# Two paces instead of one for the side work of a hybrid layer: 0.15 beside the recurrence, 0.55 from the last query projection on, where it was 0.43 throughout

## The chip, the cores and the metric

The kernel runs on one core of a Trainium2 chip. The metric is the device time of one execution in microseconds; lower is better. Engines are named as the profile names them: PE is TensorE (matmuls; PEld its weight loads), DVE is VectorE, ACT is ScalarE, POOL is GpSimd, SP is SyncE, which issues nearly all DMA.

## The reference

One inference step of a two-layer encoder over 592 tokens (16 meta tokens, 512 of a prompt, 64 of a second request that has a cache of 256 keys). Each layer computes `x + W_out(sum_b sigmoid(G_b(n)) * P_b(branch_b(n) * silu(gate_b(n))))` with `n = RMSNorm(x)`, over three branches:

```python
# A: an indexer scores all keys, each query keeps the best k, softmax over those
s_idx = relu(einsum('bthd,bsd->bths', qi, ki))
score = einsum('bth,bths->bts', wi, s_idx)       # 4 indexer heads, then top_k(score, k)
attn  = softmax over the kept keys of q.k / 8    # 8 heads of 64; k = 128, second request 80
# B: causal convolution of width 4, then a gated linear recurrence
h_t = a_t * h_(t-1) + sqrt(1 - a_t**2) * (i_t * x_t)
# C: trailing means over 2, 4, 8 and 16 frames less the token, a linear map per group
```

Queries and keys get a rotary embedding on the first quarter of each head. Keys, values, indexer keys and the states of B and C are outputs too.

## The kernel before, in words

**Projections.** The main work is a sequence of projections, emitted in a fixed order. A weight chunk of 128 x 1024 is loaded by SP (six chunks ahead at most), split by ACT and DVE into a high and a low part (`prefetch`, L190 and L191), and multiplied in three products per block of 128 (L267, `mm3`). `c_project` takes one chunk in two pieces of 296 tokens (288 in layer 1 where the meta tokens are not needed any more), 24 matmuls a piece; `psa` gives three PSUM accumulators, so a piece's result must be taken out before the third piece after it starts. After each piece it calls `spend(3 * nk * n / 2.4)`, the piece's nominal nanoseconds at the full clock: 2960 for eight blocks of 296.

**The main order in a layer**: values and indexer keys (`t_project`), two indexer queries (QI), four recurrence inputs (XB), four keys (K), four queries (Q), four gates of the recurrence (GB), the first mix (`mix(1, 0, y)`: eight sigmoid gates and the branch's output projection), four pairs of pooling input and pooling gate (XC, GC, with `pool_group`), the second mix, `side.drain()`, four gates of the attention (GA), the third mix, and the output projection. Keys and queries pass through `rope`: a shuffle on DVE (L364), two multiplications on POOL (L365, L366), an addition on DVE (L367).

**Side work** is written as generators, each of which emits some instructions and yields their cost in nanoseconds. Two queues hold them. `side_lru` (rate 0.4) has the recurrence of the four channel groups, `lru(g)`, added after each XB. `side` has the attention's work. At each `spend(ns)` a queue's credit grows by `ns * rate`, and steps are emitted as long as the credit is positive. A queue works strictly in order; `drain()` emits all that is left. This sets the order in which the program is written. A scheduler then places the instructions on each engine by this order and its own estimate of when they are ready, and an engine executes its list in order.

**`index(j)`** is the indexer for queries of block j (0 to 3: 128 prompt queries against `w = 16 + 128 * (j + 1)` keys; 4: the second request against 320). Four steps of cost `1.1 * w` compute one head's scores on PE (L445, in two PSUM tiles `pq`), which DVE (L448 for the first head, L452 after a rectifier on ACT) adds up in `sc`, of which there is one buffer. Then 16 rounds (10 for j = 4) of cost `2.1 * w + 140` each take the eight largest with `max` (L461) and strike them out with `match_replace` (L462), and a last step of cost `w` turns what was struck out into an additive `bias` (L465, two buffers).

**`attend(j)`** uses that bias: per pair of heads logits on PE (L514; L510 for j = 4), bias and maximum on DVE (L518), exponential on ACT (L524), division on POOL (L527), transposes on PE (L542), their copies on DVE and ACT, the product with the values (L557), and at the end an addition on DVE (L576). Its cost is `2.5 * w` a step, eight steps and 300 (four and 300 for j = 4). `attend_meta` (layer 0 only, cost 4700) does the meta tokens (L606 and on); it reads the rotated queries and keys.

The queue `side` gets `index(4)`, `index(0)` and `index(1)` after QI, and after Q: `attend_meta`, `attend(4)`, `attend(0)`, `index(2)`, `attend(1)`, `index(3)`, `attend(2)`, `attend(3)`. Their costs are 9,848, 7,856 and 12,848 ns, and then 4,700, 3,500, 3,180, 17,840, 5,740, 22,832, 8,300 and 10,860 ns, 76,952 in all. Before, the queue's rate is 0.43 all the time.

Of the kernel before, what the change touches and what calls it, by code (L numbers as in the profile page):

```python
# [34 lines left out]
NRAW = 3  # L35
NSPL = 3
RATE_LRU = 0.4
RATE_ATT = 0.43


class Side:
# [26 lines left out]
def build(ctx, tc, ap):  # L68
# [56 lines left out]

    side = Side(RATE_ATT)
    side_lru = Side(RATE_LRU)
# [159 lines left out]
    def c_project(ch, nk, src, pieces, evac, w=None, off=0, stride=128):  # L287

        if w is None:
            w = take(ch)  # L290
        hi, lo, _ = w[0]
        sh, sl = src
        for i, (c0, n) in enumerate(pieces):
            p = psa.tile([128, 512], F32, name="acc", tag="acc")
            pairs = []
            for k in range(nk):
                wh = hi[:, k * stride + off:k * stride + off + 128]
                wl = lo[:, k * stride + off:k * stride + off + 128]
                a, b = sh[:, k, c0:c0 + n], sl[:, k, c0:c0 + n]
                pairs += [(wh, a), (wh, b), (wl, a)]  # L300
            mm3(p[:, :n], pairs)
            evac(i, c0, n, p[:, :n])
            spend(3 * nk * n / 2.4)
# [4 lines left out]
    def layer(l, xn, x_src, last):  # L308
# [51 lines left out]
        def rope(x, c0):  # L360

            r = x.shape[0]
            t = ep.tile([128, NT], F32, name="rt", tag="e")
            nc.vector.stream_shuffle(t[:r, c0:], x[:, c0:], SWAP)  # L364
            nc.gpsimd.tensor_tensor(t[:r, c0:], t[:r, c0:], rope_s[:r, c0:], op=ALU.mult)  # L365
            nc.gpsimd.tensor_tensor(x[:, c0:], x[:, c0:], rope_c[:r, c0:], op=ALU.mult)  # L366
            nc.vector.tensor_tensor(x[:, c0:], x[:, c0:], t[:r, c0:], op=ALU.add)  # L367

        def rotated(ch, dst, pieces):
            def ev(i, c0, n, p):  # L370
                nc.scalar.activation(dst[:, c0:c0 + n], p, AF.Copy)
            c_project(ch, 8, xn, pieces, ev)
            rope(dst, pieces[0][0])
# [44 lines left out]
        def kspan(j):  # L418

            w = NM + 128 * (j + 1)  # L420
            if w <= 512:
                return [(0, w)]
            return [(0, w // 2), (w // 2, w // 2)]

        def index(j):
            sample = j == 4
            rows = 128
            q0 = NP if sample else NM + 128 * j
            w = 320 if sample else NM + 128 * (j + 1)
            sc = tmp.tile([128, 528], F32, name="sc", tag="sc")  # L430
            spans = [(0, 320)] if sample else kspan(j)
            nq = 64 if sample else 128
            for par in range(2):
                o = 64 * par
                for z in range(0, 128, nq):
                    nc.gpsimd.tensor_copy(qiz[o:o + 64, par::2, z:z + nq], QI[o:o + 64, 0:2, q0:q0 + nq])
            for h in range(4):
                q = qiz[:, h]
                for a, n in spans:
                    p = psq.tile([128, 512], F32, name="pq", tag="qk")  # L440
                    if sample:
                        nc.tensor.matmul(p[:, 0:256], lhsT=q, rhs=kx, start=True, stop=True)
                        nc.tensor.matmul(p[:, 256:320], lhsT=q, rhs=QI[:, 2, NP:NT], start=True, stop=True)
                    else:
                        nc.tensor.matmul(p[:, :n], lhsT=q, rhs=QI[:, 2, a:a + n], start=True, stop=True)  # L445
                    wh = wq[:rows, j, h:h + 1]
                    if h == 0:
                        nc.vector.tensor_scalar(sc[:rows, a:a + n], p[:rows, :n], 0.0, wh, op0=ALU.max, op1=ALU.mult)  # L448
                    else:
                        r = tmp.tile([128, 400], F32, name="rel", tag="rel")  # L450
                        nc.scalar.activation(r[:rows, :n], p[:rows, :n], AF.Relu)
                        nc.vector.scalar_tensor_tensor(sc[:rows, a:a + n], r[:rows, :n], wh, sc[:rows, a:a + n],  # L452
                                                       op0=ALU.mult, op1=ALU.add)
                yield w * 1.1
            if not sample:
                nc.gpsimd.memset(sc[0:64, w - 64:w], MASKED)  # L456
            r0 = 64 if j == 0 else 0
            rr = slice(r0, rows)
            m8 = sm.tile([128, 8], F32, name="m8", bufs=2)
            for _ in range(10 if sample else 16):  # L460
                nc.vector.max(m8[rr], sc[rr, :w])  # L461
                nc.vector.match_replace(sc[rr, :w], m8[rr], sc[rr, :w], TAKEN)  # L462
                yield w * 2.1 + 140
            b = lp.tile([128, 528], BF16, name="bias", tag="bias")
            nc.vector.tensor_scalar(b[rr, :w], sc[rr, :w], TAKEN, -1.0e30, op0=ALU.not_equal, op1=ALU.mult)  # L465
            if j == 0:
                nc.vector.memset(b[0:64, 0:w - 64], 0.0)
                nc.vector.memset(b[0:64, w - 64:w], -1.0e30)
            bias[j] = b
            yield w  # L470
# [311 lines left out]
        last_values()  # L782
        for i in range(2):
            rotated(s["c"][C_QI + i], QI[:, i], FULL)
        side.add(index(4))
        side.add(index(0))
        side.add(index(1))
# [6 lines left out]
        for i in range(4):  # L794
            rotated(s["c"][C_Q + i], QK[:, i], PIECES)
        side_lru.drain()
        if not last:
            side.add(attend_meta())
        side.add(attend(4))
# [88 lines left out]
    for t, (c0, rows) in enumerate(TILES):  # L888
        ss = sm.tile([128, 3], F32, name=f"ss{t}", bufs=1)
        for h in range(2):  # L890
            sumsq(x[t], rows, ss, h, 512 * h, 512 * h + 512)
        norm_T(x[t], rows, c0, rstd_of(ss, 2, rows), gb_t[0], *xn, xg=scale_g(x[t], rows, gb_t[0]) if t else None)
    xn = layer(0, xn, ap["xin"], False)
    layer(1, xn, x1, True)


# [73 lines left out]
```

## Time and profile before

| | us |
|---|---|
| median of three runs | 1247.98 |
| lowest and highest run | 1245.59 and 1248.61 |
| the profiled execution | 1246.41 |
| its span, first to last instruction | 1244.6 |

The profiled execution is 1.57 us below the median, and its span 1.8 us shorter than its own time. Layer 0 takes about the first half of the span, layer 1 the second. In the rows below, busy time is that of the profile: matmuls are pipelined, and a busy PE can hold more or fewer of them in the same time, so their count stands beside it. The clock column is the granted share of TensorE's clock: 1.00 is 2.4 GHz, 0.50 is 1.2 GHz.

### The profile page before, as it was taken

What the parts mean: (1) busy time and instruction counts of PE and PEld (TensorE: products, weight loads), DVE (VectorE), ACT (ScalarE), POOL (GpSimd) and SP (SyncE); (2) the same over time, 40 slices, a digit from 0 to 9 for tenths busy, and PEclk for the clock granted to TensorE, in tenths of its full rate; (3) what the DMA queues carried; (4) which work ended last, traced back from release to release, by engine and by line L of the source; (5) the groups of instructions that cost most, each with busy time, mean ns of one, the idle gap of its engine ahead of it and who ended that gap; (6) DMA issues with size and microseconds to landing.
All of it is one profiled execution on the core that took longest, in us unless ns stands there. A gap on an engine that the chain in (4) does not pass through costs nothing.

```text
span 1244.6 us, 21856 instructions
## 1 busy us (share of the span) xinstructions
PE 1214.7 (98%) x8780; PEld 1185.9 (95%) x8780; DVE 740.2 (59%) x1532; ACT 470.5 (38%) x931; POOL 333.6 (27%) x435
## 2 busy tenths in 40 slices
PE   5999899999999999999999998999999999999997
PEld 5999899999999999999999998899999999999997
DVE  6368996756964335343363789959497543344333
ACT  5336454333333322332343444543423432233223
POOL 7042453131134410011012334441221442101120
PEclk9999999999999999999999998999999999999999
DMA  8321222121232122221344212212122212222212
GB/s 270 116 90 58 101 95 68 62 75 61 68 97 69 52 94 85 86 69 68 124 152 133 68 63 96 95 68 69 52 94 77 79 52 86 78 83 85 86 52 77
DMA packets 39302, 107.39 MB, mean 86 GB/s; under 512 B 8192, under 2 KB 11328, under 8 KB 38944
## 3 DMA queue, kind: packets, MB, share of 16 engines
q1 hardware_dynamic: 39200, 105.99, 25.5%
q8 instruction: 69, 1.13, 0.4%
q14 instruction: 33, 0.27, 0.1%
HBM read 95.35 MB, written 10.09 MB: 85 GB/s over the span
## 4 chain that ended last, share of the span: by engine, by line
PE 89%; DVE 7%; issue 1%; POOL 1%; ACT 1%; DMA 1%; SPq 0%; POOLq 0%; ACTq 0%; DVEq 0%
PE acc L267 77%; PE pq L514 3%; PE pv L557 3%; PE pT L542 2%; PE pq L445 1%; DVE wl L191 1%; DVE sc L462 1%; DVE m L461 1%; DVE lxc L653 1%; PE pg L771 1%; DVE rt L364 1%; DMA xi<-xin 1%; PE pT L574 1%; PE pg L663 1%; DVE QK L367 1%
## 5 line engine op out<-in xcount | busy, mean ns | idle before, releaser
L267 PE MATMUL acc<-xh,wh 128*128 128x296 f32 (+1 forms) x1728 | 530.2, 307 | 0.5 <-DVE e L705 0.5
L267 PE MATMUL acc<-xh,wl 128*128 128x296 f32 (+1 forms) x1728 | 523.6, 303 | 0.0
L267 PE MATMUL acc<-xl,wh 128*128 128x296 f32 (+1 forms) x1728 | 520.1, 301 | 0.0
L267 PEld LDWEIGHTS acc<-xh,wh 128*128 128x128 f32 x1728 | 327.8, 190 | 4.6 <-DVE e L705 0.7
L267 PEld LDWEIGHTS acc<-xl,wh 128*128 128x128 f32 x1728 | 327.9, 190 | 3.3
L191 DVE TENSOR_TENSOR wl<-wr,wh 128x1024 fp32r<-128x1024 f32 (+1 forms) x158 | 211.6, 1341 | 199.2 <-ACT wh L190 196.1
L267 PEld LDWEIGHTS acc<-xh,wl 128*128 128x128 f32 x1728 | 326.4, 189 | 1.8
L190 ACT ACTIVATE wh<-wr 128x1024 fp32r<-128x1024 f32 (+1 forms) x158 | 166.1, 1053 | 251.0 <-PE acc L267 222.2
L267 PE MATMUL acc<-yh,wh 128*128 128x296 f32 (+1 forms) x384 | 116.9, 304 | 0.0
L267 PE MATMUL acc<-yl,wh 128*128 128x296 f32 (+1 forms) x384 | 115.6, 301 | 0.0
L267 PE MATMUL acc<-yh,wl 128*128 128x296 f32 (+1 forms) x384 | 115.6, 301 | 0.0
L527 POOL TENSOR_SCALAR lpa<-lpa,mn 128x128 f32<-128x128 f32 (+4 forms) x72 | 81.6, 1134 | 109.6 <-DVE mn L526 101.1
L267 PE MATMUL acc<-wh,ml 128*128 128x256 f32 (+2 forms) x320 | 89.4, 281 | 0.0
L267 PE MATMUL acc<-wh,mh 128*128 128x256 f32 (+2 forms) x320 | 88.5, 280 | 0.0
L267 PE MATMUL acc<-wl,mh 128*128 128x256 f32 (+2 forms) x320 | 88.5, 280 | 0.0
L461 DVE MAX8 m<-sc 64x8 f32<-64x144 f32 (+4 forms) x148 | 74.6, 504 | 3.6 <-POOL sc L456 0.7
L267 PEld LDWEIGHTS acc<-yl,wh 128*128 128x128 f32 x384 | 72.2, 188 | 1.3 <-issue 0.2
L267 PEld LDWEIGHTS acc<-yh,wl 128*128 128x128 f32 x384 | 72.2, 188 | 1.2 <-issue 0.4
L267 PEld LDWEIGHTS acc<-yh,wh 128*128 128x128 f32 x384 | 72.3, 188 | 1.0
L462 DVE MATCH_REPLACE8 sc<-m,sc 64x144 f32<-64x144 f32 (+4 forms) x148 | 72.5, 490 | 0.2
L744 POOL TENSOR_TENSOR e<-m,e 128x592 f32<-128x592 f32 (+1 forms) x16 | 23.1, 1446 | 184.4 <-DVE e L738 184.4
L524 ACT ACTIVATE lpa<-lpa,mn 128x144 f32<-128x144 f32 (+4 forms) x72 | 41.2, 572 | 75.3 <-DVE mn L518 75.2
(204 smaller groups left out, 1748.1 us busy)
## 6 DMA issues: line engine op xcount, KB each, us to landing
wr<-wc SPq DMA_DIRECT2D x108, 512.0 KB, 3.3
wr<-wb SPq DMA_DIRECT2D x24, 512.0 KB, 3.2
wr<-wo SPq DMA_DIRECT2D x16, 512.0 KB, 3.5
kT<-QK SPq DMA_DIRECT2D x2, 1184.0 KB, 4.2
xi<-xin SPq DMA_DIRECT2D x8, 256.0 KB, 8.2
wr<-wv SPq DMA_DIRECT2D x4, 512.0 KB, 6.6
v_p<-VI SPq DMA_DIRECT2D x16, 128.0 KB, 2.1
xo<-xin SPq DMA_DIRECT2D x8, 256.0 KB, 3.1
```

The costliest lines, as they stand in the source:

```text
L190: nc.scalar.activation(h[:, :size], r[:, :size], AF.Copy)
L191: nc.vector.tensor_sub(lo[:, :size], r[:, :size], h[:, :size].bitcast(F32))
L267: nc.tensor.matmul(out, lhsT=a, rhs=b, start=(i == 0), stop=(i == n - 1))
L364: nc.vector.stream_shuffle(t[:r, c0:], x[:, c0:], SWAP)
L461: nc.vector.max(m8[rr], sc[rr, :w])
L462: nc.vector.match_replace(sc[rr, :w], m8[rr], sc[rr, :w], TAKEN)
L514: nc.tensor.matmul(p[:, :n], lhsT=qz[u // 2 % 2][:, u % 2], rhs=QK[:, 4 + u // 2, a:a + n], start=True, stop=True)
L524: nc.scalar.activation(t[:, :w], t[:, :w], AF.Exp, bias=mn[:, i:i + 1], scale=-1.0, accum_out=mn[:, 2:3])
L527: nc.gpsimd.tensor_scalar(t[:, :wm], t[:, :wm], mn[:, 3:4], None, op0=ALU.mult)
L542: nc.tensor.transpose(ps[:, k], t[:, 128 * k:128 * k + 128], ident)
L557: nc.tensor.matmul(pvs[i // 2][:, i % 2], lhsT=val(k, i), rhs=pt[:, k], start=(k == 0 and i % 2 == 0), stop=(k == nb - 1), skip_group_chec ...
L744: nc.gpsimd.tensor_tensor(e[:, C0:], m[:, j, C0:], e[:, C0:], op=ALU.add)
```

## The change

The queue `side` gets a rate of its own for the stage between the indexer queries and the last query projection, 0.15, and a rate of 0.55 from there on. What is emitted, its order within a queue, the recurrence's rate and the main order stay as they are.

```diff
 RATE_LRU = 0.4
-RATE_ATT = 0.43
+RATE_ATT = 0.55
+RATE_EARLY = 0.15
...
         for i in range(2):
             rotated(s["c"][C_QI + i], QI[:, i], FULL)
+        side.rate = RATE_EARLY
         side.add(index(4))
         side.add(index(0))
         side.add(index(1))
...
             rotated(s["c"][C_Q + i], QK[:, i], PIECES)
         side_lru.drain()
+        side.rate = RATE_ATT
         if not last:
             side.add(attend_meta())
         side.add(attend(4))
```

## Rows read from the trace of the kernel before

**Rows 1.** The page: busy us by engine, and the clock in 40 slices

```profile
PE 1214.7 (98%) x8780; PEld 1185.9 (95%) x8780; DVE 740.2 (59%) x1532; ACT 470.5 (38%) x931; POOL 333.6 (27%) x435
PEclk9999999999999999999999998999999999999999
```

**Rows 2.** Stretches: length; busy us (instructions) of PE, PEld, DVE, ACT, POOL; clock; DMA

```profile
125.00:150.00 25.00, 21.89 (x145) 20.92 (x144) 23.75 (x57) 11.88 (x19) 11.22 (x9) 0.97 0.27 97
175.00:200.00 25.00, 23.17 (x188) 22.28 (x187) 24.59 (x70) 9.55 (x22) 9.99 (x16) 1.00 0.23 76
475.00:500.00 25.00, 25.00 (x185) 25.00 (x184) 12.67 (x18) 8.64 (x15) 0.00 (x0) 1.00 0.24 85
750.00:775.00 25.00, 21.74 (x140) 21.03 (x139) 24.23 (x51) 11.32 (x19) 10.91 (x11) 0.86 0.31 112
775.00:800.00 25.00, 22.94 (x160) 21.70 (x159) 24.51 (x54) 13.32 (x20) 12.12 (x15) 1.00 0.30 97
```

**Rows 3.** Waits of PE: waiting <- waited for: us, times, longest us

```profile
PE pq L445 <- DVE sc L448: 6.4, 2, 3.3
PE pq L606 <- DVE QK L367: 1.8, 1, 1.8
PE pq L510 <- POOL VI L484: 1.6, 1, 1.6
```

**Rows 4.** Stretches at and behind the lower clock, as rows 2

```profile
148.40:151.90 3.50, 3.50 (x16) 3.50 (x16) 3.50 (x8) 0.40 (x1) 0.88 (x2) 0.51 0.45 150
151.90:155.40 3.50, 3.50 (x28) 3.50 (x27) 3.50 (x3) 2.07 (x4) 3.50 (x2) 1.00 0.00 0
759.40:766.30 6.90, 5.53 (x21) 5.29 (x22) 6.87 (x10) 1.69 (x4) 3.08 (x2) 0.51 0.44 165
766.30:773.20 6.90, 6.90 (x54) 6.90 (x53) 6.90 (x11) 2.24 (x5) 3.83 (x7) 1.00 0.08 12
```

**Rows 5.** DVE lines: shapes xcount | busy us, mean ns; last: 172:198 alone

```profile
L461 DVE MAX8 m<-sc 64x8 f32<-64x144 f32 x32 | 9.8, 307 | 1.1
L462 DVE MATCH_REPLACE8 sc<-m,sc 64x144 f32<-64x144 f32 x32 | 9.5, 295 | 0.2
L462 DVE MATCH_VALUE_LOAD sc<-m,sc 128x8 f32 x116 | 10.1, 87 | 2.2
L461 DVE MAX8 m<-sc 128x8 f32<-128x272 f32 x32 | 13.9, 434 | 0.3
L462 DVE MATCH_REPLACE8 sc<-m,sc 128x272 f32<-128x272 f32 x32 | 13.5, 422 | 0.0
...
L461 DVE MAX8 m<-sc 128x8 f32<-128x272 f32 x9 | 3.9, 428 | 0.0
```

**Rows 6.** Stretches, as rows 2; then the rounds' lines of 304:377

```profile
75.00:172.00 97.00, 93.89 (x651) 90.95 (x651) 86.26 (x181) 52.20 (x88) 37.74 (x45) 0.98 0.23 78
172.00:198.00 26.00, 24.17 (x194) 23.28 (x193) 25.91 (x73) 11.36 (x23) 10.05 (x14) 1.00 0.28 91
304.00:343.00 39.00, 39.00 (x281) 38.52 (x280) 36.60 (x74) 11.98 (x22) 7.68 (x12) 1.00 0.21 72
304.00:377.00 73.00, 73.00 (x505) 70.18 (x504) 57.31 (x118) 24.84 (x50) 20.35 (x31) 1.00 0.25 81
...
L462 DVE MATCH_REPLACE8 sc<-m,sc 128x528 f32<-128x528 f32 x15 | 10.4, 692 | 0.0
L461 DVE MAX8 m<-sc 128x8 f32<-128x528 f32 x14 | 9.9, 706 | 0.1
```

**Rows 7.** Timeline: start us, us, engine, line; DVE, then POOL

```profile
124.69 2.04 DVE L653 SCALAR_TENSOR_TENSOR lxc<-CH,prm,lxc 128x595 f32<-128x595 f32 x1
126.76 0.31 DVE L461 MAX8 m<-sc 64x8 f32<-64x144 f32 x1
129.15 0.84 DVE L653 SCALAR_TENSOR_TENSOR lxc<-CH,prm,lxc 128x595 f32<-128x595 f32 x1
...
126.06 1.99 POOL L366 TENSOR_TENSOR QK<-QK,rope_c 128x592 f32<-128x592 f32 x1
```

## The prediction, made before the changed kernel was timed

> **What bounds the kernel now.** I read the page first: TensorE is busy for 98% of the span, and the strip of the granted clock is at its top but for one slice [rows 1]. A busy TensorE of pipelined matmuls says little by itself, so the next view is the table of stretches, 25 us each. In a stretch with nothing beside the projections TensorE starts 185 matmuls in 25 us and never idles. Four stretches differ: it idles 3.11 us (125 to 150) and 1.83 us (175 to 200) in layer 0, and 3.26 and 2.06 us in the same places of layer 1, 10.26 us together [rows 2]. In all four VectorE is busy 23.75 to 24.59 of 25 us. So VectorE bounds the kernel there, and TensorE everywhere else.
>
> The waits of TensorE say what it stood for: index scores (L445) for the score tile that L448 on VectorE writes, twice, 6.4 us; the meta attention (L606) for the rotary add L367 on VectorE, 1.8 us; the sample attention (L510) for a GpSimd copy that comes behind the same add, 1.6 us [rows 3]. L448 can't write before the index before it has let go of the single `sc` tile, and that one's rounds stand in VectorE's queue among the recurrence, the rotary steps and the weight splits. After the two L445 waits the clock is at its lower level (1.2 GHz, 0.51 as a mean): 16 matmuls in 3.5 us where the next 3.5 us have 28, and 21 in 6.9 us where the next 6.9 us have 54 [rows 4]. Half of the busy time at the lower level is lost: 3.50 / 2 = 1.75 us and 5.53 / 2 = 2.8 us. What VectorE's overload costs now is thus 10.26 + 1.75 + 2.8 = 14.8 us of the profiled execution. That is all that pacing can give back: the late stretches hold no such gap, and the work of TensorE is the same in both kernels.
>
> **The change, part by part.** (a) *Rate 0.15 from the index queries on.* A piece of a projection is worth 24 x 296 / 2.4 = 2960 ns, so it now pays 444 ns of side work instead of 1273. Twelve projections (24 pieces) stand between there and the last query projection: 71,040 ns. At 0.43 they paid 30,547, and the three indices cost 9,848 (sample), 7,856 (index 0) and 12,848 (index 1), 30,552 in all: just everything. At 0.15 they pay 10,656: the sample's index, and the four score steps of index 0 with one round or two. About 19,600 ns, the rest of index 0 and all of index 1, go behind the last query projection.
>
> What leaves VectorE's early stretch: of index 0, 16 rounds of 307 + 295 + 87 = 689 ns, 11.0 us; of index 1, 16 rounds of 434 + 422 + 87 = 943 ns, 15.1 us, of which 7 rounds run before the last query projection's end at 172 us and 9 behind it; with some 4 us of score sums (an estimate) I put 21 us on this stretch [rows 5]. VectorE is busy 86.26 of the 97 us from 75 to 172 [rows 6]; 65 us stay, 70% of the 92 us that remain without the idle time and the slow clock. The two L445 waits are of index 1 and can't stand there any more. Their 3.11 + 1.75 and 3.26 + 2.8 = 10.9 us go. GpSimd's queue loses four copies into `qiz` (two an index) there, which by the code wait for the scores before them and hold up the rotary multiplications behind; this helps the rotary steps to come in time. The side steps issue no DMA, so on SP's queue nothing is passed.
>
> One rule speaks against counting so much. While GpSimd did rotary multiplications (one of 1.99 us), a recurrence step on VectorE that takes 0.84 us a little later took 2.04, and a MAX8 in between its usual 0.31 [rows 7]. The Trainium skill, page "SBUF — State Buffer", section "Who interferes with whom", says that a VectorE instruction with two SBUF inputs and a GpSimd instruction that reads SBUF exclude each other, and one with a single SBUF input doesn't. The trace agrees. By it the lengthened steps are the recurrence's and the rotary's and stay where they are; the rounds that leave were never lengthened, so no more than their own time is freed. The 21 us above take only that; without the rule one could hope for the excess too, 2.04 - 0.84 = 1.2 us for each step so lengthened, which would free VectorE further and leave the sum in (d) as it is.
>
> (b) *What is late next.* Behind the last query projection come the four GB projections, 26 us. An equal stage without side work, the GA projections, keeps VectorE busy 12.67 of 25 us [rows 2]: 13 us for GB. To that come index 0 (11 us of rounds and some 2 of sums) and, by its credit of 1,628 ns a piece, not quite half of index 1, 8 us: 34 us of VectorE work in the 26 us of TensorE work plus about 3 for the moved score matmuls. The recurrence's tail adds up to 3 (an estimate). Out of the stage go the meta and sample attentions. So VectorE falls 5 to 8 us behind. A main stream with three PSUM accumulators bears a delay of two pieces: 2 x 24 matmuls at 25 / 185 = 135 ns, 6.5 us, before TensorE waits for an evacuation (L705). And index 1's scores again need the `sc` tile of index 0. The bounds for what is lost here: nothing (the same stage had VectorE 25.91 of 26 us busy before [rows 6] and lost little but the waits L606 and L510, which now fall away, since both attentions come 19,628 / 0.55 = 35.7 us of projections later), and the stalls of before in full, 10.9 us. I take 4 us, one wait of about 2 us per layer, as in this stage before (1.83 and 2.06 us), the nearest rows [rows 2].
>
> (c) *Rate 0.55.* A piece pays 1,628 ns instead of 1,273. The queue behind the last query projection holds 76,952 + 19,628 ns; at 0.55 that takes 176 us of nominal projection time, at 0.43 the smaller 76,952 took 179, of 213 us up to the drain. So the side work ends at the same place and the drain holds nothing. But index 3 now lies wholly in the pooling stage (credit from its first to its last projection). In layer 0 14 or 15 of its 16 rounds ran there already; VectorE was busy 57.31 of 73 us, 20.3 of them these rounds, and TensorE had no idle time at all [rows 6]. One or two rounds more of 706 + 692 + 87 = 1.49 us and the score sums add some 6 us: 63 of 73, still covered on the mean. In layer 1, whose index 3 starts earlier by its credit, more rounds move in, up to the same sum. Cover gone, each such wait costs 2 to 6 us; I take 0, since no row shows one at this load.
>
> (d) *Sum.* -10.9 (the L445 waits and their clock) - 3.9 (L606 and L510) + 4 (new waits) + 0 = -10.8 us. The profiled execution took 1246.41 us, 1.6 below the median of 1247.98 and 1.8 above its own span; it becomes 1235.6, the median 1237.
>
> **The rivals.** *The stall moves.* Index 1's scores stand in TensorE's queue where a plan expects `sc` to be free; VectorE in the GB stage is again overloaded, and the wait recurs at full price. Then only L606 and L510 are won, 3.9 us, or a little of the rest: 1244. For it: it is the same pair of tiles and the same engine, near full load. Against: few GpSimd multiplications run there, so that VectorE keeps its usual durations, and the indices 2 and 3, which hold the same pair at the same kind of load, show no wait.
>
> *Slower: a backlog that the accumulators don't bear.* Raised pace puts rounds ahead of main evacuations, in the GB stage and again where index 3 meets the pooling chains. It decides from a backlog over two pieces, 6.5 us. Its price is that of the stalls of before, 4.9 us (3.11 + 1.75) to 6.1 us (3.26 + 2.8) each, the slow clock included; one in each of the two stages of each layer makes 22 us, against 14.8 won: +7, 1255. For it: 34 us of work on 29 us. Against: from 304 to 343 us VectorE was busy 36.60 of 39 us, and TensorE all the time [rows 6].
>
> *Nothing.* If the program's order on each engine came from readiness alone and the pace only broke ties, the traces would be alike: 1248. Against it: by its credit index 3 starts in the last gates of the first mix, and in the trace its rounds start there too, a round or two before the pooling stage [rows 6].
>
> **How the numbers follow.** Forecast 0.60: 1237, own range 1231 to 1243. Stall moves 0.20: 1241 to 1247. Slower 0.12: 1250 to 1260. Nothing 0.08: 1246 to 1250. The low end is all 14.8 us won with nothing late, 1233, less some restart time around each gap that I didn't count: 1230. The high end reaches over "nothing" to the start of the slower case: 1250. About 0.1 stays above and 0.04 below. A measurement of this kernel can tell about 0.3%, 3.7 us, from no change. Faster than 1244.2: 0.58 of the forecast and half of the second, 0.68. Within: the other half, "nothing" and a little, 0.20. Slower: 0.12.
>
> **What would show it.** (a) is right if VectorE between 75 and 172 us is near 70% busy, TensorE has no idle time there and the clock is at its upper level from 75 to 800 us. (b) is right if the waits L445 on L448, L606 on L367 and L510 on L484 are gone or moved behind the last query projection, with at most 2 us per layer. A wait L445 on L448 of 3 us there is the first rival; waits of L267 on L705, or of L771 on the pooling chain, of several us are the second. (c) is right if L576 of the last attention stays before the drain and the pooling stage has no idle time. I am wrong in the sum if the gaps vanish and the span doesn't follow.

## The result: slower, and the profile after

| | before | after |
|---|---|---|
| median, us | 1248.20 | 1255.64 |
| lowest and highest | 1245.59 to 1249.64 | 1254.08 to 1256.35 |
| span of the profiled execution | 1244.6 | 1252.4 |

Six executions of each. After over before is 1.0063, 95% interval 1.0052 to 1.0074: 7.4 us slower, where 11 us faster was forecast. Lines of the kernel after stand one lower in the file than those of before (L445 is L446, L705 is L706, L738 is L739); in the kernels with one more tile, below, one further (L447, L707).

The table of stretches of the kernel after (columns as in [rows 2]):

```profile
75.00:172.00 97.00, 94.95 (x665) 92.30 (x665) 74.71 (x118) 54.27 (x89) 39.19 (x48) 1.00 0.26 87
125.00:150.00 25.00, 25.00 (x179) 24.51 (x178) 18.98 (x24) 13.10 (x21) 11.82 (x9) 1.00 0.31 112
150.00:175.00 25.00, 22.95 (x159) 21.75 (x157) 19.67 (x33) 14.20 (x23) 14.75 (x19) 1.00 0.30 97
175.00:200.00 25.00, 21.40 (x148) 20.59 (x148) 23.44 (x66) 8.13 (x16) 1.55 (x2) 1.00 0.22 70
750.00:775.00 25.00, 25.00 (x180) 24.34 (x179) 18.38 (x23) 16.07 (x26) 13.69 (x12) 1.00 0.32 113
775.00:800.00 25.00, 22.19 (x141) 21.56 (x140) 22.08 (x47) 11.46 (x20) 9.46 (x15) 0.86 0.29 97
800.00:825.00 25.00, 23.50 (x172) 23.00 (x172) 23.32 (x64) 8.15 (x16) 1.71 (x4) 1.00 0.23 77
300.00:377.00 77.00, 77.00 (x526) 73.88 (x525) 61.34 (x134) 27.31 (x61) 18.75 (x33) 1.00 0.24 78
788.60:795.50 6.90, 5.99 (x25) 5.99 (x26) 6.46 (x19) 0.00 (x0) 1.01 (x4) 0.51 0.22 63
795.50:802.40 6.90, 6.90 (x51) 6.74 (x51) 6.42 (x19) 2.74 (x5) 0.00 (x0) 1.00 0.20 58
```

The stretches 125 to 150 and 750 to 775 us, in which [rows 2] show 3.11 and 3.26 us of idle TensorE, are full now. The stage of the GB projections behind them is not: 2.05 + 3.60 us of idle time in layer 0, 2.81 + 1.50 us in layer 1, and there the clock falls to its lower level (0.51: 25 matmuls in 6.9 us, 51 in the next 6.9), which loses half of 5.99 us. Together 5.65 + 7.3 = 13.0 us. Of these, 10.1 us fall between the first and the last GB matmul (159.9 to 192.6 us, 776.8 to 809.6 us); the rest are waits for the score tile up to 5 us on either side.

TensorE's waits in the kernel after (columns as in [rows 3]; the larger ones, without those for weight splits and at the layers' ends, which both kernels have):

```profile
PE acc L268 <- DVE e L706: 5.6, 3, 2.8
PE pq L446 <- DVE sc L449: 2.8, 3, 1.5
PE pT L543 <- POOL lpa L528: 2.0, 3, 0.8
...
PE pv L552 <- ACT pt L547: 1.6, 3, 0.6
PE pq L446 <- ACT rel L452: 1.5, 1, 1.5
PE pq L511 <- DVE mn L519: 1.4, 2, 0.9
PE pv L552 <- DVE pt L545: 1.1, 2, 0.7
```

Two groups. The first, second and fifth lines are the GB stage: accumulators not emptied (L706), score tiles not free. The rest, 6.1 us, are waits inside the sample attention (L511 to L552). An attention's own chain can only stop TensorE where it has nothing else to do, and before it always had. The same two stretches in the two kernels, before first:

```profile
209.00:227.00 18.00, 18.00 (x128) 17.26 (x127) 6.74 (x24) 7.91 (x24) 7.03 (x16) 1.00 0.18 58
822.00:843.00 21.00, 21.00 (x145) 19.42 (x144) 9.51 (x30) 10.03 (x28) 7.31 (x17) 1.00 0.14 51
```

```profile
209.00:227.00 18.00, 14.71 (x130) 12.76 (x130) 15.29 (x63) 5.91 (x20) 6.85 (x13) 1.00 0.09 30
822.00:843.00 21.00, 17.60 (x126) 16.04 (x126) 19.34 (x69) 7.14 (x20) 7.52 (x14) 1.00 0.15 51
```

In the kernel after, TensorE starts not one projection matmul between 212.75 and 226.72 us, and none between 830.6 and 842.0 us. The timeline at the end of the first of these, with lines left out at the dots (start, duration, engine, line):

```profile
225.23 0.94 PE L552 MATMUL pv<-pt,CH 128*128 128x128 f32 x6 [0.46 <-DVE pt L545]
...
226.20 1.21 DVE L739 SCALAR_TENSOR_TENSOR m<-e,acc 128x296 f32<-128x296 f32 x3
226.72 0.19 PEld L268 LDWEIGHTS acc<-yh,wh 128*128 128x128 f32 x1 [0.28 <-DVE m L739]
226.72 0.40 PE L268 MATMUL acc<-yh,wh 128*128 128x296 f32 x1
```

The last product of the sample attention, L552, reads CH. Right behind its end VectorE takes out three accumulators at once (L739, x3), and only then does the projection go on. L739 writes `m`, the first mix's sums. The code says why it may not come sooner: `m` (L719) is the fourth tile asked of the pool `big`, which has three buffers (QK, VI, CH), and it gets that of CH. CH holds the second request's cached keys and values, and the sample's values, which the sample attention reads. So `m` can't be written before attend(4) is over. In the kernel before, the last L551 of attend(4) ended at 211.2 us and the first L738 came at 221.7 us, for the projection's sake. Indices 0 and 1 stand ahead of attend(4) in the queue of both kernels; with the lower early pace most of them is emitted only behind the last query projection, and attend(4), behind them, falls into the first mix.

### The profile page after: what moved, and what is told of

Its sections match the earlier page's. It is cut to its first block, busy times and chain, and to the rows that moved or that the text cites. A ratio compares the mean times of both kernels' runs of the same rounds, so it can differ in the third digit from the quotient of the medians.

```text
span 1252.4 us, 21853 instructions
## 1 busy us (share of the span) xinstructions
PE 1216.4 (97%) x8780; PEld 1185.4 (95%) x8780; DVE 739.4 (59%) x1532; ACT 471.9 (38%) x931; POOL 329.2 (26%) x435
## 4 chain that ended last, share of the span: by engine, by line
PE 80%; DVE 12%; issue 3%; POOL 2%; ACT 2%; DMA 1%; SPq 0%; POOLq 0%; DVEq 0%; ACTq 0%
PE acc L268 69%; PE pq L515 3%; PE pv L558 3%; DVE wl L192 3%; DVE sc L463 2%; DVE m L462 2%; PE pT L543 1%; PE pq L446 1%; POOL rt L366 1%; POOL QK L367 1%; DVE lxc L654 1%; DVE rt L365 1%; PE pg L772 1%; PE pT L575 1%; DMA xi<-xin 1%
```

## The experiments

All times are medians in us beside runs of the kernel before on the same chip; ratios carry their 95% interval. The theories in the expectations: M, the wait of `m` for the sample attention; D, VectorE's load of rounds in the GB stage; S, that moved work costs as much where it goes. R is, in the first four runs, that the raised pace as such is the cost, and from the run with pace 0 on, that the first evacuations in the GB stage are late for what stands ahead of them in VectorE's list, the recurrence's tail above all.

**The two rates, one at a time.**

```diff
-RATE_ATT = 0.55
+RATE_ATT = 0.43
```

> The change's first half alone: pace 0.15 beside the recurrence, 0.43 from the last query projection on. Theory M (the first mix's sums go into the buffer of the big pool that the sample attention still reads; the sample attention now stands behind indices 0 and 1, so TensorE has nothing but that attention's chain to run): the wait stays or grows, since the queue comes later still, and the early waits are won: 1250 to 1260 us. Theory D (VectorE overloaded in the stage of the recurrence's gates by the indices that moved there): a lower pace there takes about half of that stage's 7 us a layer away. M and D together 1250 to 1256. Rival R (it is the raised pace 0.55 that costs): 1236 to 1243.

Measured 1259.63 against 1247.74, ratio 1.0089 [1.0072, 1.0106]: slower still. The raised pace is not what costs; with the lower one attend(4) comes later yet, and `m` with it (first written at 230.9 and 847.4 us, where the changed kernel has 226.2 and 841.5). Most of the extra loss in layer 0 is the clock: it was at its lower level from 216.8 to 227.1 us, behind a wait of 1.4 us (L511 on L610); TensorE was busy for 9.93 us of that, half of which, 5.0 us, is lost, and layer 1 begins 5.8 us later than in the changed kernel. Theory D's half fell too: the waits on L706 were not halved (7.2 us in five; in the changed kernel 5.6 us in three).

```diff
-RATE_EARLY = 0.15
+RATE_EARLY = 0.43
```

> The second half alone: pace 0.43 beside the recurrence, 0.55 from the last query projection on. The three indices are paid for before that projection, as in the kernel before. M and D: no index stands ahead of the sample attention, so both costs are away and the early waits of the kernel before stay: 1245 to 1251 us. R: 1252 to 1260.

Measured 1251.16, ratio 1.0027 [1.0015, 1.0039], just above what M and D allow and below R's range. The two L446 waits of before stand unchanged (6.4 us), and a wait of 1.3 us for the pooling chain is new (an accumulator for ScalarE's L712, near 413 us): with the indices early *and* the raised pace, the side work does press on the pooling stage a little.

**The buffer.** The cached keys and values and the sample's values get a tile of their own, which the pool `big` doesn't hand on; nothing else changes.

```diff
-        CH = big.tile([128, 5208], F32, name="CH", tag="big")
-        kc = CH[:, 0:1024].rearrange("p (t c) -> p t c", t=4)
+        CH = big.tile([128, 2648], F32, name="CH", tag="big")
+        CA = lay.tile([128, 2560], F32, name="CA")
+        kc = CA[:, 0:1024].rearrange("p (t c) -> p t c", t=4)
...
```

> The changed kernel (0.15 and 0.55), but the cached keys and values that the sample attention reads stand in a tile of their own, not in the one of the big pool whose buffer the first mix takes over. M: TensorE's stretches from 209 to 227 us and from 822 to 843 us get projections between the attention's steps, 5 to 6 us less in each layer: 1243 to 1247 us, and what remains over 1240 is D's. D alone or R alone: 1253 to 1258.

Measured 1242.44, ratio 0.9957 [0.9942, 0.9972], 13.2 us less than the changed kernel and just under M's range. The two stretches are full, with more matmuls:

```profile
209.00:227.00 18.00, 18.00 (x146) 17.44 (x147) 14.38 (x48) 5.20 (x12) 2.33 (x3) 1.00 0.23 70
822.00:843.00 21.00, 21.00 (x163) 20.79 (x162) 16.36 (x58) 7.97 (x21) 7.68 (x14) 1.00 0.23 76
```

In the changed kernel `m` is first written at 226.20 us, right behind attend(4)'s last product; with the own tile at 210.6 us, before that attention's first product (226.9 us), and likewise in layer 1 (822.7 and 832.4 us). The wait is gone.

The projections' matmuls come in one order in all these kernels, so the start of the same one can be compared between traces. The 2,705th (behind layer 0's drain, with all side work of the layer done) starts 4.0 us later after than before, and 1.7 us earlier with the own tile; the 6,686th, behind the drain of layer 1, 7.8 us later and 3.7 us earlier. The wait of `m` is thus worth 5.7 + 5.8 = 11.5 us. The control is the same tile in the kernel before:

```diff
-        CH = big.tile([128, 5208], F32, name="CH", tag="big")
+        CH = big.tile([128, 2648], F32, name="CH", tag="big")
+        CA = lay.tile([128, 2560], F32, name="CA")
...
```

> The kernel before (pace 0.43 throughout) with the cached keys and values of the second request and the sample's values in a tile of their own, as in the run of the changed kernel with that tile. Theory M (in the changed kernel the first mix's sums wait for the sample attention, which still reads CH; in the kernel before that attention was over some 11 us before the sums began): there is nothing to win here, 1246 to 1250, ratio 0.998 to 1.002, and the waits for index scores (3.1 and 3.3 us) stand as they were. Rival P (the own tile helps by itself, whatever the pace, because CH comes free earlier or the scheduler places the work otherwise): 1234 to 1243, and the 13 us that the tile won in the changed kernel say nothing about its cause.

Measured 1243.80 against 1247.91, ratio 0.9970 [0.9961, 0.9980]: between the two theories. The own tile is worth some 4 us at the old pace as well. Its trace doesn't say where: the early waits stand (3.1 and 3.3 us), the 2,705th and the 6,686th matmul are 0.2 us later and 0.6 us earlier than before, but the two traced executions don't stand for the medians: this one took 1245.18 us, 1.4 above its median, and that of the kernel before 1246.41, 1.5 below the 1247.91. So of the 13.2 us at most 13 are the wait of `m`, and some 9 if the tile is worth the same 4 at either pace, which no run shows; the traces say 11.5. Where the 4 come from stays open.

**The order.** The same wait, removed without a tile: attend_meta and attend(4) are queued ahead of indices 0 and 1.

```diff
         side.add(index(4))
-        side.add(index(0))
-        side.add(index(1))
...
         side.add(attend(4))
+        side.add(index(0))
+        side.add(index(1))
         side.add(attend(0))
```

> The changed kernel, but the queue from the last query projection on starts with the meta and the sample attention and has indices 0 and 1 behind them (index 4 alone beside the recurrence). M: the buffer is free before the first mix, 1242 to 1248 us. D: the indices overload a later stretch, where the first mix leaves VectorE more room, so that a part of the 7 us a layer in the gates' stage goes too: down to 1238. R: 1252 to 1258.

Measured 1241.63, ratio 0.9948 [0.9933, 0.9963]. `m` is written at 215.5 us, behind attend(4)'s last product (203.9). So two different edits, after which attend(4) no longer holds up `m`, give 13 and 14 us. This one does more than that, though: the GB stage's waits fall (L706 from 5.6 to 0.9 us, L446 from 4.3 to none), and the meta and sample attentions now stand so close behind the rotary steps that they wait for those, 3.5 us (L607 on L368) and 2.3 us (L511 on L485), with the clock at its lower level for 3.4 and 6.8 us beside these waits. Against the changed kernel 10 us of idle time and 3 us of clock go, and 6.7 and some 4 come, so that about 2 of the 14 us are not the wait of `m`.

**The GB stage.** All runs from here on have the own tile, but for one control. What is left with it:

```profile
PE acc L268 <- DVE e L707: 6.9, 4, 2.9
...
PE pq L447 <- DVE sc L450: 3.1, 3, 1.5
...
PE pq L447 <- ACT rel L453: 1.5, 1, 1.5
```

First, no side work emitted in that stage, and `RATE_ATT` 0.6 behind it:

```diff
-        side.rate = RATE_ATT
+        side.rate = 0.0
...
+        side.rate = RATE_ATT
         mix(1, 0, y)
```

> The changed kernel with the cache in a tile of its own, and no side work at all emitted during the four GB projections (pace 0 there), 0.6 from the first mix on. Theory D (what is left in the GB stage is VectorE's overload: rounds of indices 0 and 1 stand ahead of the evacuations L707, and the three accumulators fill up): the losses of that stage go, 6.8 us in layer 0 and 7.7 us in layer 1 with its lower clock, and the mix bears the delayed indices: 1242.4 - 14.5 = 1228, 1226 to 1233; TensorE busy all of 157 to 200 us and 780 to 815 us. Rival S (the overload moves with the work: the same rounds now stand ahead of the first mix's evacuations, or index 3 falls on the pooling chains): the GB waits go and others of 2 to 6 us a layer come behind 200 us and behind 820 us, 1238 to 1246. Rival R (GB waits have another cause, such as the recurrence's tail or the weight splits): waits on L707 stay between 157 and 200 us, 1239 to 1245.

Measured 1241.66, ratio 0.9954 [0.9938, 0.9971]: the same as with 0.55 (0.9957), within the noise. The waits on L707 at 171, 176 and 783 us stay, as theory R has it, but the run can't speak against D, for VectorE's rounds were not gone:

```profile
L463 DVE MAX8 m<-sc 64x8 f32<-64x144 f32 x16 | 4.9, 308 | 0.5
```

That is the count from 157 to 200 us, all 16 rounds of index 0, as many as in the changed kernel. A pace sets where a step is written in the program; the scheduler pulled these rounds forward all the same: by the credits all but one are written behind the stage, and in the trace they run from 169 to 195 us, between its evacuations. Index 0's scores, which they read, were written ahead of the stage. What it moved are index 1's scores.

Next, an early rate between the two, with 0.5 behind; in the second kernel the lower rate holds to the end of the GB stage.

```diff
-RATE_ATT = 0.55
-RATE_EARLY = 0.15
+RATE_ATT = 0.5
+RATE_EARLY = 0.25
```

> The changed kernel with the cache in a tile of its own and the paces 0.25 and 0.5 in place of 0.15 and 0.55: by the credits index 0 is emitted beside the recurrence (17,704 of 17,760 ns), index 1 behind the last query projection. Theory D: VectorE has 76 of 92 us beside the recurrence and bears it; the GB stage has 13 us of its own and up to 15 us of index 1's rounds in 26 us, so about one wait of 1 to 2 us a layer is left there: 1230 to 1236. Rival S: the early waits on the score tile come back (3 us each), or the GB stage loses what it lost, 1239 to 1245.

> As the run with paces 0.25 and 0.5 and the own tile, but the lower pace of 0.25 holds to the end of the GB projections and 0.5 begins with the first mix. Theory D: VectorE in the GB stage has 13 us and some 7 us of index 1, 20 of 26 us: no wait there, 1226 to 1232, at or under the run without side work in that stage. Rival S: waits come behind 200 us in place of those, 1236 to 1244.

Measured 1248.73 and 1249.61, ratios 1.0012 [1.0003, 1.0021] and 1.0015 [1.0006, 1.0025]: 6 to 7 us lost against 0.15, the same with either rate in the GB stage, and above the ranges of both theories. The stretch and the waits of the first of them:

```profile
125.00:172.00 47.00, 39.99 (x269) 37.73 (x269) 43.63 (x89) 25.07 (x39) 21.17 (x20) 0.99 0.28 101
...
PE pq L447 <- DVE sc L450: 11.1, 2, 6.8
...
PE pg L665 <- DVE lxc L655: 4.0, 2, 2.3
```

One index of the prompt beside the recurrence is enough to bring the score tile's wait back (4.3 us at 171, 6.8 us at 789 us). So theory D's budget, 76 of 92 us and therefore no wait, was wrong, and the low early rate is the good half of this change.

Then the other suspect, the recurrence's tail ahead of the first GB evacuations. In the changed kernel TensorE is done with the first GB piece of layer 1 at 780.3 us, and VectorE takes it out (L706) at 789.0, 8.7 us later; in layer 0 it is 163.4 and 171.0 us, 7.6 us. VectorE just before; L680 to L683 are the recurrence's tail:

```profile
786.17 0.77 DVE L680 SCALAR_TENSOR_TENSOR lT<-lT,lthi 128x595 f32<-128x595 f32 x1
786.86 0.36 DVE L453 SCALAR_TENSOR_TENSOR sc<-rel,wq,sc 128x144 f32<-128x144 f32 x1
787.14 1.24 DVE L682 TENSOR_TENSOR_SCAN CH<-la,lT 128x528 f32<-128x528 f32 x1
788.31 0.32 DVE L683 TENSOR_TENSOR_SCAN CH<-la,prm,lT 128x64 f32<-128x64 f32 x1
788.66 0.31 DVE L462 MAX8 m<-sc 64x8 f32<-64x144 f32 x1
789.00 0.45 DVE L706 SCALAR_TENSOR_TENSOR e<-e,acc 128x288 f32<-128x288 f32 x1
```

The longest of VectorE's waits from 75 to 172 us, before and after:

```profile
DVE sc L452 <- ACT rel L451: 4.2, 3, 2.5
DVE VI L367 <- POOL VI L366: 3.1, 1, 3.1
```

```profile
DVE QK L368 <- POOL QK L367: 12.9, 5, 3.1
```

After, VectorE stands 12.9 us before the rotary additions until GpSimd has done the multiplications, and the recurrence's steps stand behind it in the same list. Before, rounds stood ahead of each addition and filled that time. Two ways to get the tail out of the way: a faster recurrence, or half of GpSimd's multiplications on VectorE.

```diff
-RATE_LRU = 0.4
+RATE_LRU = 0.5
```

> The changed kernel with the cache in a tile of its own, and the recurrence's rate 0.5 in place of 0.4, so that its last group is emitted some three pieces earlier and nothing of it is left for the drain behind the last query projection. Theory R (the waits of TensorE on L707 at 171, 176, 783 us stay without any side work emitted in that stage, so they come from what VectorE has in its list ahead of the first GB evacuations: the recurrence's tail L677 to L684, which is late because VectorE has idled there for GpSimd's rotary multiplications): these waits go, 3.2 us in layer 0 and 4.2 us and 1.7 us of clock in layer 1: 1242.4 - 9 = 1233, 1230 to 1237. Rival D (VectorE is simply overloaded in the GB stage): no change, 1240 to 1244. Rival E (the recurrence brought forward collides with the rotary steps and the scores in the early stretch): new waits of 2 us or more between 75 and 157 us, 1242 to 1248.

```diff
-            nc.gpsimd.tensor_tensor(t[:r, c0:], t[:r, c0:], rope_s[:r, c0:], op=ALU.mult)
+            nc.vector.tensor_tensor(t[:r, c0:], t[:r, c0:], rope_s[:r, c0:], op=ALU.mult)
```

> The changed kernel with the cache in a tile of its own, and of the two rotary multiplications on GpSimd the first (L367, 8 times 1.67 us between 75 and 172 us) on VectorE instead, so that GpSimd's share of a rotary step is one multiplication that can start as soon as the projection is copied out. Theory R: VectorE's idle time for GpSimd (12.9 us in five waits of L369 between 75 and 172 us) goes for the most part, 8 to 10 multiplications of some 0.8 us come to VectorE in its place, the recurrence's tail ends earlier and the waits on L707 behind it go: 1233, 1230 to 1238. Rival D: VectorE has 8 us more to do, the waits on L707 grow: 1243 to 1250. No effect, 1240 to 1244, if the tail is late for a reason of its own (its chain over ScalarE).

Measured 1238.97, ratio 0.9931 [0.9916, 0.9946], and 1236.48, ratio 0.9906 [0.9890, 0.9923]. The first lies between R's range and D's, the second in R's. In both the 16 rounds are still in the GB stage, and the waits on L707 fall from 6.9 us to 1.6 and 2.8 us: theory R holds for most of them. The first GB piece is taken out 2.7 and 4.0 us after it is done with the faster recurrence (layers 0 and 1), 6.1 and 4.7 us with the multiplication moved, where it was 7.7 and 8.8 us with the own tile alone. The faster recurrence pays part of it back with waits of the recurrence's matmuls (L665, 5.0 us in four, between 123 and 142 us and in the like place of layer 1), as rival E said. With the multiplication moved, VectorE's longest wait for a rotary multiplication is 1.4 us, and something else is won. The recurrence's step L653, mean ns of the twelve of layer 0, before, after and with the multiplication moved:

```profile
L653 DVE SCALAR_TENSOR_TENSOR lxc<-CH,prm,lxc 128x595 f32<-128x595 f32 x12 | 11.9, 990 | 0.2
```

```profile
L654 DVE SCALAR_TENSOR_TENSOR lxc<-CH,prm,lxc 128x595 f32<-128x595 f32 x12 | 14.3, 1194 | 0.2
```

```profile
L655 DVE SCALAR_TENSOR_TENSOR lxc<-CH,prm,lxc 128x595 f32<-128x595 f32 x12 | 10.0, 831 | 0.1
```

In layer 1 the three means are 1092, 1013 and 828 ns: the moved multiplication shortens the steps in both layers, while the paces lengthened them in one and shortened them in the other.

The control moves the same multiplication in the kernel before, where VectorE is the full engine.

```diff
-            nc.gpsimd.tensor_tensor(t[:r, c0:], t[:r, c0:], rope_s[:r, c0:], op=ALU.mult)
+            nc.vector.tensor_tensor(t[:r, c0:], t[:r, c0:], rope_s[:r, c0:], op=ALU.mult)
```

> The kernel before (pace 0.43 throughout), and only the first rotary multiplication on VectorE in place of GpSimd. Theory R with its second half (at the old pace VectorE between 75 and 172 us is full, 86 of 97 us, and hardly waits for GpSimd there: 3.1 us in all, against 16.0 us in the changed kernel): here the moved multiplications are 8 times 0.8 us of work more on the engine that bounds the stretch, so the waits L445 on L448 grow or stay: 1246 to 1256. Rival G (GpSimd's multiplications, which lengthen the recurrence steps beside them, are what costs VectorE its time at either pace): VectorE's steps shorten, the waits shrink: 1236 to 1243.

Measured 1248.23 against 1246.50, ratio 1.0013 [1.0003, 1.0023]: nothing won, the waits on the score tile grow from 6.4 to 8.3 us. GpSimd was not the limit at the old pace; the lower pace made it one.

The moved multiplication and pace 0 in the GB stage together, 0.6 behind it:

```diff
-            nc.gpsimd.tensor_tensor(t[:r, c0:], t[:r, c0:], rope_s[:r, c0:], op=ALU.mult)
+            nc.vector.tensor_tensor(t[:r, c0:], t[:r, c0:], rope_s[:r, c0:], op=ALU.mult)
...
-        side.rate = RATE_ATT
+        side.rate = 0.0
...
+        side.rate = RATE_ATT
         mix(1, 0, y)
```

> The changed kernel with the cache in a tile of its own, the first rotary multiplication on VectorE, no side work emitted during the GB projections and 0.6 from the first mix on. What TensorE still waits for in the GB stage with the first two alone is 1.3 us on L707 and 2.3 us on index scores in layer 0, 1.6 and 1.3 us in layer 1, 6.5 us together. Theory D for this rest (side work in the GB stage holds up the evacuations and scores once the recurrence is out of the way): the most of it goes, 1236.5 - 5 = 1231.5, 1229 to 1234. Rival S (the delayed indices cost as much in the first mix and behind it, as without the rotary change, where the same pacing won 0.8 us): 1235 to 1239.

Measured 1236.62, ratio 0.9915 [0.9895, 0.9934]: no change from the rotary alone. The number lies in rival S's range, but no wait has moved behind the stage, as S has it: 4.8 us of waits on L707 stay there, and the 16 rounds are there again (4.9 us of MAX8), as at pace 0 before.

Last, a GB stage that is meant to be really empty: indices 0 and 1, and all that follows them, are put into the queue behind it (0.6 from there), so that not even the scores exist.

```diff
         side.add(index(4))
-        side.add(index(0))
-        side.add(index(1))
...
             split_y(y, g, e)
+        side.add(index(0))
+        side.add(index(1))
+        if not last:
+            side.add(attend_meta())
+        side.add(attend(4))
...
         mix(1, 0, y)
```

> The changed kernel with the cache in a tile of its own; indices 0 and 1 and all that follows are put into the queue only behind the GB projections (0.6 from there). Pace 0 in that stage alone did not empty it: there 16 rounds of index 0, whose scores stood ahead of it, still ran on VectorE between 157 and 200 us. Here not even the scores exist yet, so no round can. Theory D (rounds ahead of the evacuations L707 make the three accumulators fill up): all waits on L707 go, in layer 0 at 171 and 176 us and in layer 1 at 783 us too, 5.4 + 6.5 us of the run with pace 0: 1230 to 1234. Theory R (the first of these waits come from the recurrence's tail and the rotary steps, which stand ahead of the first evacuations with or without the rounds): the waits at 171 and 783 us stay at 1.3 to 3 us each, only the later ones of 0.5 to 0.9 us go: 1237 to 1240. Rival S: the delayed indices cost in the first mix what the GB stage wins: 1240 to 1246.

> The same, and the first rotary multiplication on VectorE. Theory R and D together (the recurrence's tail accounts for the first waits in the GB stage, index 0's rounds for those behind it): TensorE has no wait over 0.3 us between 75 and 200 us and between 700 and 815 us, 4.4 and 3.6 us less than with the rotary change alone: 1236.5 - 7 = 1229, 1227 to 1232. Rival S (the delayed indices cost as much behind 200 us and 815 us): 1234 to 1239.

Measured 1230.99, ratio 0.9866 [0.9851, 0.9881], and with the rotary multiplication on VectorE 1227.17, ratio 0.9837 [0.9820, 0.9853]. The stretch from 157 to 200 us with the own tile alone, with the empty stage, and with both:

```profile
157.00:200.00 43.00, 37.32 (x258) 35.81 (x259) 38.66 (x91) 17.39 (x30) 10.78 (x17) 1.00 0.27 88
```

```profile
157.00:200.00 43.00, 42.35 (x307) 41.63 (x305) 30.70 (x55) 19.94 (x33) 11.99 (x15) 1.00 0.32 105
```

```profile
157.00:200.00 43.00, 43.00 (x316) 42.86 (x315) 30.17 (x60) 19.55 (x33) 6.12 (x10) 1.00 0.28 93
```

Both theories had their share. The first round now runs at 196.7 us, behind the stage's last evacuation (188.8). The empty stage leaves waits of 0.6 us (170 us) and 1.1 us (777 us) on L707, not the 1.3 to 3 us that R alone would keep; the rounds and the tail add up in one list, and taking away either gets the evacuations nearly in time. With both gone TensorE is not idle at all between 75 and 230 us, nor from 300 to 377 us, where the delayed work now runs. This kernel is 20.4 us faster than the kernel before and, by the two ratios, some 28 us faster than the change.

## Why the prediction was wrong

**(a) was right in what it won.** The L445 waits and their clock went in both layers (25.00 of 25 us). Of the 21 us that were to leave VectorE, 16.5 did in layer 0. The stretch from the first recurrence input's matmul to the first GB matmul, before and after:

```profile
69.70:166.40 96.70, 93.58 (x642) 90.91 (x641) 83.35 (x172) 49.25 (x84) 37.01 (x45) 0.98 0.23 77
69.00:159.90 90.90, 90.36 (x634) 87.95 (x633) 66.88 (x106) 48.26 (x81) 35.73 (x40) 1.00 0.25 84
```

In layer 1 it was 17.8 us (84.05 to 66.29). The stretch from 75 to 172 us, by which the prediction wanted to judge, shows only 11.5 us (74.71 of 97 us, 77%, not 70%), since the kernel after is 6.5 us ahead there and has more of its GB stage in it. The prediction took 172 us for the end of the last query projection; the GB matmuls begin at 166.4 us, and by then 4 rounds of index 1 had run, not 7. Its 4 us of score sums were 1.8 us in layer 0 and 2.7 us in layer 1.

The prediction took the rule of the Trainium skill, page "SBUF — State Buffer", section "Who interferes with whom", to mean that the lengthened steps stay as they are. The trace bears the rule out: with half of the multiplications gone none of the 24 steps L653 took over 0.86 us, with all there some took up to 2.04 us. How many did changed little, five before (two in layer 0, three in layer 1) and six after (four and two), but not in the same places. What (a) missed is VectorE's own idle time for GpSimd, hidden under rounds before, which now showed: 12.9 us.

**(b) is the step that failed**, twice. Its term for new waits behind the last query projection, 4 us, measured 13.0 us, beyond its upper bound of 10.9; 10.1 us of them lie in the GB stage itself. It counted VectorE's work against the stage's length (34 us on 29), and the list didn't run so: VectorE was late at the stage's very start, 7.6 and 8.7 us after the first piece, more than the 6.5 us that it took the accumulators to bear, since the recurrence's tail was late; over the stage it was busy 38.85 of 43 us (38.66 with the own tile). Moved rounds (the empty GB stage, −11.5 us beside the own tile alone) and that tail (the faster recurrence and the moved multiplication, −3.5 and −6 us) are both in it. The tail runs over ScalarE too, and no run changed that part of it. And its sentence "Out of the stage go the meta and sample attentions" booked the move as a gain of 3.9 us without asking who waits for the sample attention. That it reads CH, and that `m` takes CH's buffer, stands in the code; it was never put to the trace. That wait, 11.5 us, is missing from the sum altogether.

**(c) was right.** Between 300 and 377 us TensorE is busy 77.00 of 77 us with VectorE at 61.34, and the side work ends before the drain.

**(d) with measured terms:** −10.9 − 3.9 + 13.0 + 11.5 = +9.7 us. The 6,686th projection matmul is 7.8 us late and the medians differ by 7.4 us; some 2 us remain unaccounted for.

**The rivals.** "Slower: a backlog that the accumulators don't bear" named the sign, the wait (L267 on L705) and one of its two places, with 11 us there against 8.6 measured on that wait (5.6 us and 3.0 us of clock); its other place, index 3 at the pooling stage, showed nothing, and the first mix, which no rival had, took its part. That its 1255 us is the time measured is therefore luck. "The stall moves" is in the trace too, small (L446 on L449, 2.8 us in three). "Nothing" fell, though its idea, that readiness and not the pace sets VectorE's order, holds for the rounds (16 of them at pace 0).

## What to carry to other kernels

Before a step is moved back in the order, list not only who waits for its result but who takes over the buffers that it reads: a rotating pool hands them on, and the writer then waits for the moved step. Work taken off a full engine is not all won: what it was hiding (here VectorE's waits for GpSimd) becomes visible, and the next things in that engine's list come late, so look at the first evacuation behind the stretch. A pace on emission did not keep ready work out of a stage here; leaving its inputs unwritten did.

## What the runs showed of the hardware beyond that

Waits of one length cost different clock. In layer 1's GB stage TensorE waited 2.8 us in the changed kernel, and the lower level then held for some 6.9 us (0.51, above). With the own tile it waited 2.9 us, and the lower level held for 3.4 us; at pace 0 it waited 2.9 us at the same place and the clock stayed up:

```profile
784.66:788.07 3.41, 3.41 (x16) 3.41 (x15) 3.21 (x9) 0.00 (x0) 0.76 (x2) 0.50 0.00 0
```

```profile
783.00:790.00 7.00, 5.35 (x38) 5.12 (x39) 6.56 (x19) 0.63 (x2) 0.79 (x2) 1.00 0.22 78
```

Why they differ the runs don't tell. Executions of one kernel differ too: the four at pace 0 had mean granted clocks of 0.995 to 0.999. The price of the clock behind such a wait, half of 0, 3.41 or 5.99 us, leaves an estimate like the one above uncertain by up to 3 us.
